# Balanced branches on TensorE, one scatter for four experts' third places, a tenth chunk buffer and another order at the end

## The chip, the cores and the metric

The kernel runs on one core of a Trainium2 chip. The metric is the time of one execution on the device in microseconds; three runs of the kernel before gave 696.25, 698.2 and 699.58 us, median 698.2.

## What is computed

The input is one sequence of 256 tokens with 1024 features, in float32. A first block of two hybrid layers is followed by a second block: a mixer (state-space scan and attention), a layer norm, a mixture of experts and a last layer norm. Only the mixture of experts and the last norm matter here. Each token goes to two of the four experts of one of four groups, 16 experts in all, and an expert is a gated product of 1024 to 512 and back:

```python
def _hier_moe(h, rg_w, rg_b, re_w, re_b, w_gate, w_up, w_down):
    ...
    weights = g_val[:, None] * e_val
    expert_id = g_idx[:, None] * EXPERTS_PER_GROUP + e_idx
    combine = jnp.sum(jax.nn.one_hot(expert_id, N_EXPERTS, dtype=jnp.float32) * weights[..., None], axis=1)
    out = jnp.zeros((bsz * s, d), jnp.float32)
    for e in range(N_EXPERTS):
        act = jax.nn.silu(hf @ w_gate[e]) * (hf @ w_up[e])
        out = out + combine[:, e:e + 1] * (act @ w_down[e]).astype(jnp.float32)
    ...
    # in second_block, behind it:
    h = _layer_norm(DEEPNORM_ALPHA * h + ffn, ln2_g[l], ln2_b[l])
```

## The kernel before, in words

The last third of the program is the expert stage. An expert's tokens are given places: 64 in a first part, 32 in a second, called the third 32 places, and more in a far branch (`further`, L1823) that is entered when any expert has over 96. A one-hot matrix `oh` of a group (128 tokens x 384 places for each half of the sequence: four experts' first 64 places each, then four times 32) is made by `picks` on VectorE. `gather` multiplies the normed tokens, split into two parts, by it and so makes `xg`, the transposed inputs of a group's four experts; `spread` transposes `oh` into `oT` (two ScalarE copies, three blocks: the places of experts 0 and 1, of 2 and 3, and the third 32 of all four), and `scatter` multiplies `oT` by the weighted outputs and adds to the four PSUM banks `acc` of the result. `weights` makes the routing weight of each place by 12 small fp32 products.

Expert e (e = 4q + j, group q, place j in it) goes through these steps. `gate_up` (L1701, called from it) multiplies 32 places by two weight chunks of 2 MB into one PSUM bank, 32 matmuls; a second bank for places 32 to 63 and a third for 64 to 95 are made under `tc.If` on the expert's count (L1726, L1728). `activate` adds the halves, applies Silu and multiplies on ScalarE and VectorE (L1740 to L1744), bank by bank. `turn` (L1762) transposes the result and VectorE copies it to `aT`. `down` multiplies by a third chunk (L1708 for 64 places, L1701 for 32), one expert later: the down of e stands behind the gate_up of e+1. `take` (L1800 to L1803, L1770) copies the result to `y`, and `split_all` (L1810, L1811) weighs it and splits it into two parts for the scatter, for two experts at a time. If the count is over 64 (L1779), `down` first turns the third 32 places in a small transpose, multiplies them, takes, splits and scatters them half by half, and then goes on with the 64 places. From the timeline's rows e4 and e8 have three banks, e0, e2, e6, e10 and e12 two, the others one, and no expert has over 96 places.

The order is written out by hand in `experts`, and each engine runs its instructions in that order. At j = 1 `spread` and the scatter of the group before stand behind gate_up; at j = 2 `weights` of the next group; at j = 3 the scatter of the first pair and `gather_all` for the next group. A `tc.If` without an Else raises on the skipped path the same semaphores that the taken path would have raised, after the engine's own work is done. Weight chunks come over one DMA queue issued by SyncE into a ring of nine buffers (`add_ring`, `load`, `give_back`); a buffer's next load is issued once its last reader is through. At the end stand `further`, the down of e15, the last scatter and the layer norm (L1968 and on).

Of the kernel before, what the change touches and what calls it, by code (L numbers as in the profile page):

```python
# [21 lines left out]
HALF = 512  # L22
# [224 lines left out]
class Net:  # L247
# [1254 lines left out]
    def router(self):  # L1502
# [57 lines left out]
        self.comb = K.tile([P, NT, 16], F32, name="comb")  # L1560

        def weights():
# [7 lines left out]
            by_group(self.comb, ee)  # L1570
        self.pos = K.tile([P, NT, 16], F32, name="pos")
# [22 lines left out]
        nc.scalar.activation(w[:, 0:4:3], w[:, 0:4:3], AF.Exp)  # L1594
        V.tensor_mul(self.pos, ps[:, 0:32].rearrange("p (t e) -> p t e", t=NT), asg)
        self.cnt = K.tile([P, 17], I32, name="cnt")
# [4 lines left out]
        V.tensor_reduce(self.cnt[:, 16:17], self.cnt[:, 0:16], axis=AX, op=OP.max)  # L1601
# [28 lines left out]
    def weights(self, q, oh):  # L1630

        nc, o = self.nc, oh.bitcast(F32)
# [5 lines left out]
        w = self.mw.tile([P, 3, 5], F32, name="wq", bufs=2)  # L1638
        nc.vector.tensor_mul(w[:, :, 0:4], ps[:, 0:12].rearrange("p (c j) -> p c j", c=3), self.c("own", 3, 4))
        nc.vector.tensor_reduce(w[:, :, 4], w[:, :, 0:4], axis=AX, op=OP.add)  # L1640
        return w[:, :, 4]
# [28 lines left out]
    def scatter_all(self, oT, last=False):  # L1670
        for h in range(2):
            self.scatter(oT, [a[:, HALF * h:HALF * h + HALF] for a in self.y], h, last=last)

    def residual(self):
# [17 lines left out]
        self.y2 = [self.mw.tile([P, HALF], F32R if n else F32, name=f"y2{n}") for n in range(3)]  # L1692
        nc.gpsimd.memset(self.y[0], 0.0)

# [15 lines left out]

    def gate_up(self, e):
# [10 lines left out]
        banks = self.gus = [self.gu, self.mbank("s"), self.mbank("s")]  # L1722
        if e + 1 < N_EXP:
            self.count(e + 1)
        self.product32(banks[0], w, KT, x(64 * j))
        with tc.If(self.n[e] > 32):  # L1726
            self.product32(banks[1], w, KT, x(64 * j + 32))
            with tc.If(self.n[e] > 64):  # L1728
                self.product32(banks[2], w, KT, x(256 + 32 * j))
        self.give_back(*rs)  # L1730

    def activate(self, e):
# [13 lines left out]
        with tc.If(self.na[e] > 32):  # L1746
            act(self.gus[1], self.sg[32:64, :], 1)
            with tc.If(self.na[e] > 64):
                act(self.gus[2], self.sg2[0:32, :], 1)

    def count(self, e):
        E = mybir.EngineType
# [273 lines left out]
```

## Time and profile before

| what | value |
|---|---|
| median of three runs | 698.2 us |
| profiled execution | 696.77 us |
| its span in the profile | 695.0 us |
| TensorE busy | 626.3 us, 90% |
| VectorE busy | 451.6 us, 65% |
| ScalarE busy | 306.8 us, 44% |
| mean DMA rate | 236 GB/s |
| mean granted TensorE clock | 0.96 of full speed |

The span begins with the first instruction and ends with the last output's landing; 1.8 us of the execution's time lie around it. All engines run side by side, so a busy share says little by itself. What is to be read is, stage by stage, which engine has no idle time left, and for each of its waits who ended it. The granted clock is that of TensorE's array: at half clock the same matmul row takes nearly twice as long.

### The profile page before, as it was taken

Reading aid. Unit: us, or ns where it says so; the run is one execution under the profiler, and the core shown is the slowest. Engines: PE = TensorE matmul, PEld = TensorE weight load, DVE = VectorE, ACT = ScalarE, POOL = GpSimd, SP = SyncE. Lnnn points to the kernel's source line nnn. Section 1 sums busy time; section 2 is a strip of 40 time slices with the busy share of each in tenths; the row PEclk is TensorE's granted clock in tenths of the full one; section 3 lists DMA queues with packets and bytes.
Section 4 is the critical chain, followed back from the end, with each engine's and each line's share of the span. In section 5 each row is a group of like instructions: output and inputs, shape, how many; then the busy total and the mean of one; then the engine's idle time right before and its main releaser. Section 6 shows DMA issues by size and latency. Waiting matters only on the chain. (4 is left out here: it accounts for less than half of the span.)

```text
span 695.0 us, 11796 instructions
## 1 busy us (share of the span) xinstructions
PE 626.3 (90%) x4466; PEld 443.4 (64%) x4466; DVE 451.6 (65%) x1064; ACT 306.8 (44%) x601; POOL 6.3 (1%) x28
## 2 busy tenths in 40 slices
PE   7999999899899999999999989878979897999762
PEld 4799878688897887898888866523533442363211
DVE  5898767777986777796859877634334433443426
ACT  6764554567545645534646424323332332233321
POOL 1000000000000000000000000000000000000001
PEclk9999999999999999999989998989998998899986
DMA  8956223234452033663305169799999999799821
GB/s 318 426 182 241 112 104 122 92 126 177 165 220 103 5 122 122 273 256 123 123 27 198 56 241 387 282 379 430 421 413 379 371 421 426 280 428 413 333 66 60
DMA packets 15920, 163.68 MB, mean 236 GB/s; under 512 B 1888, under 2 KB 2144, under 8 KB 6624
## 3 DMA queue, kind: packets, MB, share of 16 engines
q1 hardware_dynamic: 15552, 161.84, 58.4%
q8 instruction: 48, 0.79, 0.4%
q10 hardware_dynamic: 288, 0.79, 0.3%
q14 instruction: 32, 0.26, 0.1%
HBM read 161.57 MB, written 1.05 MB: 234 GB/s over the span
## 5 line engine op out<-in xcount | busy, mean ns | idle before, releaser
L318 ACT ACTIVATE whi<-wchunk 128x1024 fp32r<-128x1024 f32 (+2 forms) x103 | 107.4, 1043 | 94.6 <-PE pj L420 49.5
L319 DVE TENSOR_TENSOR wlo<-wchunk,whi 128x1024 fp32r<-128x1024 f32 (+2 forms) x103 | 123.0, 1197 | 18.8 <-ACT whi L318 18.5
L419 PE MATMUL pj<-xh,whi 128*128 128x256 f32 (+1 forms) x440 | 126.8, 289 | 0.0
L420 PE MATMUL pj<-xl,whi 128*128 128x256 f32 (+1 forms) x440 | 126.3, 287 | 0.0
L421 PE MATMUL pj<-xh,wlo 128*128 128x256 f32 (+1 forms) x440 | 125.2, 285 | 0.0
L419 PEld LDWEIGHTS pj<-xh,whi 128*128 128x128 f32 (+1 forms) x440 | 82.5, 188 | 3.2 <-issue 2.2
L420 PEld LDWEIGHTS pj<-xl,whi 128*128 128x128 f32 (+1 forms) x440 | 82.7, 188 | 2.9 <-issue 1.9
L421 PEld LDWEIGHTS pj<-xh,wlo 128*128 128x128 f32 (+1 forms) x440 | 82.7, 188 | 1.8 <-issue 1.6
L1701 PE MATMUL gu<-wchunk,xg 128*32 128x512 f32 x512 | 60.1, 611 | 0.8 <-issue 0.5
L1741 DVE TENSOR_TENSOR tg<-tg,gu 64x256 f32<-64x256 f32 x32 | 13.2, 412 | 46.5 <-ACT tg L1740 46.4
L420 PE MATMUL pj<-wlo,xh 128*128 128x512 f32 (+2 forms) x112 | 40.3, 360 | 1.6 <-DVE wlo L319 1.6
L419 PE MATMUL pj<-whi,mh 128*128 128x512 f32 x96 | 38.5, 404 | 2.6 <-ACT mh L510 2.1
L420 PE MATMUL pj<-wlo,mh 128*128 128x512 f32 x96 | 38.1, 398 | 2.5 <-DVE wlo L319 2.5
L419 PE MATMUL pj<-whi,xh 128*128 128x512 f32 (+2 forms) x112 | 39.1, 355 | 1.1 <-ACT whi L318 1.1
L421 PE MATMUL pj<-whi,xl 128*128 128x512 f32 (+2 forms) x112 | 39.9, 356 | 0.0
L421 PE MATMUL pj<-whi,ml 128*128 128x512 f32 x96 | 37.5, 400 | 0.0
L1701 PEld LDWEIGHTS gu<-wchunk,xg 128*32 128x32 f32 x512 | 15.6, 112 | 32.9 <-issue 32.0
L1667 PE MATMUL acc<-y,oT 128*128 128x512 f32 (+1 forms) x80 | 26.9, 470 | 9.1 <-ACT y L1810 7.7
L1740 ACT ACTIVATE tg<-gu 64x256 f32<-64x256 f32 x32 | 12.1, 379 | 52.1 <-PE gu L1701 31.6
L553 ACT ACTIVATE prob<-bank,smst 128x128 f32<-128x128 f32 (+1 forms) x64 | 26.1, 419 | 18.4 <-DVE smst L551 18.4
L1708 PE MATMUL dn<-wchunk,aT 128*64 128x512 f32 x112 | 28.9, 663 | 4.8 <-PEq L1779 2.8
L1701 PE MATMUL mbs<-wchunk,xg 128*32 128x512 f32 x288 | 32.2, 592 | 0.0
(404 smaller groups left out, 1045.1 us busy)
## 6 DMA issues: line engine op xcount, KB each, us to landing
wchunk<-wstream SPq DMA_DIRECT2D x67, 2048.0 KB, 11.2
wchunk<-wstream SPq DMA_DIRECT2D x12, 512.0 KB, 14.2
wchunk<-wstream SPq DMA_DIRECT2D x2, 1536.0 KB, 9.8
wchunk<-wstream SPq DMA_DIRECT2D x2, 1024.0 KB, 8.4
wchunk<-wstream SPq DMA_DIRECT2D x4, 436.0 KB, 5.6
wchunk<-wstream SPq DMA_DIRECT2D x1, 1744.0 KB, 6.6
wchunk<-xt SPq DMA_DIRECT2D x4, 256.0 KB, 5.3
X<-x SPq DMA_DIRECT2D x4, 256.0 KB, 5.8
```

Of the source, the lines that this page charges most:

```text
L318: nc.scalar.activation(hi, w, AF.Copy)
L319: nc.vector.tensor_sub(lo, w, hi.bitcast(F32))
L419: mm(out, ah, bh, start=start, stop=False)
L420: mm(out, ah, bl, start=False, stop=False)
L421: mm(out, al, bh, start=False, stop=stop)
L553: nc.scalar.activation(p[:, e, j, :N], S[e][:, j, :], AF.Exp, bias=nm[:, e, j:j + 1], accum_out=sm[:, e, j:j + 1])
L1667: self.nc.tensor.matmul(self.acc[t][h], oT[r, t * P:(t + 1) * P], y[1 + i], start=False, stop=last and i == 1, **at)
L1701: self.nc.tensor.matmul(out[r:r + 32, :], lhs(k), w(k)[:, HALF * i:HALF * i + HALF], start=(k < 2), stop=(k >= n - 2), tile_position=(0, r))
L1708: self.nc.tensor.matmul(out[64 * i:64 * i + 64, :], lhs(k), w(k)[:, HALF * i:HALF * i + HALF], start=(k == 0), stop=(k == n - 1), tile_pos ...
L1740: nc.scalar.activation(tg[0:64, 0, s], b[64:128, s], AF.Copy)
L1741: V.tensor_add(tg[0:64, 0, s], tg[0:64, 0, s], b[0:64, s])
```

## The change

- On TensorE every `If` in `gate_up`, `down` and the new `third` gets an Else. It holds one-column products of zeros with the same weight buffers (`none`), so that both paths raise equal signals. Counts are loaded for TensorE apart from ScalarE and VectorE, which no longer take part in TensorE's branches.
- `turn` transposes 96 rows at once instead of 64, and ScalarE makes the copy `aT`, in two buffers.
- The third 32 places: `third` multiplies them behind the turn of the next expert, `take_third` puts them into their rows of `y2` (one tile for a group), and at j = 1 of the next group `split_third` and one scatter treat all four experts' thirds, if any expert of the group has over 64. For TensorE, an Else with four small products stands in for the scatter. Those of e14 and e15 and of the last group go to `further`, which is now entered over 64 in the last group or over 96 anywhere.
- `spread` moves from j = 1 to behind the first activation for e0, and to j = 2, behind gate_up, in later groups. The second scatter of a group stays at j = 1. `take(e - 1)` stands behind `turn(e)`; the chunk is given back behind the third; the scatter of the first pair stands behind the turn.
- `weights` is done for each group at the end of `gather_all`, with a split pair `comb2` in fp32r. `picks` moves to j = 2. The Silu table is loaded in the router.
- Three buffers are added to the ring instead of two: ten in all.
- At the end: the clears of WARM[3] go to `dn`, straight behind the gate_up of e15; `further` stands behind the down and the take of e15; the take splits each half when it has it; the statistics run by halves.

```diff
@@ router
+        nc.scalar.activation(mv[:, 0, 6:7], mv[:, 0, 0:1], AF.Silu)
...
+        V.tensor_reduce(self.cnt[:, 17:21], self.cnt[:, 0:16].rearrange("p (q j) -> p q j", q=4), axis=AX, op=OP.max)
+        V.scalar_tensor_tensor(self.cnt[:, 16:17], self.cnt[:, 16:17], -32.0, self.cnt[:, 20:21], op0=OP.add, op1=OP.max)
@@ weights
-                nc.tensor.matmul(ps[:, 4 * c:4 * c + 4], o[:, t, P * c:P * c + P], self.comb[:, t, 4 * q:4 * q + 4],
+                nc.tensor.matmul(ps[:, 8 * c:8 * c + 8], oh[:, t, P * c:P * c + P], self.comb2[:, t, q],
@@ gate_up
+    def none(self, b, w):
+        self.nc.tensor.matmul(b[:, 0:1], self.zero, w.bitcast(BF16)[:, 1:2], start=True, stop=True)
...
-        with tc.If(self.n[e] > 32):
+        with tc.If(self.n[e] > 32) as more:
             self.product32(banks[1], w, KT, x(64 * j + 32))
-            with tc.If(self.n[e] > 64):
+            with tc.If(self.n[e] > 64) as much:
                 self.product32(banks[2], w, KT, x(256 + 32 * j))
+            with much.Else():
+                none(2)
+        with more.Else():
+            none(1)
+            none(2)
@@ turn
-        aT = self.mw.tile([P, 4, 64], F32, name="aT")
-        nc.vector.tensor_copy(aT.rearrange("p a n -> p (a n)"), ps[:, 0:256])
+        aT = self.mw.tile([P, 4, n], F32, name="aT", bufs=2)
+        nc.scalar.activation(aT.rearrange("p a n -> p (a n)"), ps[:, 0:4 * n], AF.Copy)
@@ third, take_third, split_third
+        b = self.mbank("s")
+        with self.tc.If(self.n[e] > 64) as more:
+            self.product32(b, lambda k: wd[:, k, :], 4, lambda k: aT[:, k, 64:96])
+        with more.Else():
+            self.none(b, wd[:, 0, 0:1])
...
+        with self.tc.If(n > 64):
+            self.nc.scalar.activation(self.t3, b[64:128, :], AF.Copy)
+            for h in range(2):
+                self.add32(b, h, self.y2[32 * j:32 * j + 32, HALF * h:HALF * h + HALF])
...
+        for h in range(2):
+            self.split_rows([self.y2] + y, slice(0, P), slice(HALF * h, HALF * h + HALF), self.wq[q][:, 2:3])
@@ experts, for each e
-            if j == 1:
-                if q:
-                    self.scatter_all(oT[:, 1, :])
+            if j == 1 and q:
+                self.scatter_all(oT[:, 1, :])
+            if j == 2 and q:
                 oT = self.spread(self.oh)
...
             self.activate(e)
+            if e == 0:
+                oT = self.spread(self.oh)
+            if last:
+                for _ in range(WARM[3]):
+                    self.clear(self.dn)
+            a0, aT = aT, self.turn(e)
             if e and not last:
                 self.take(e - 1)
+                b = self.third(e - 1, a0, wd(w))
+                self.give_back(r)
+                self.take_third(e - 1, b, self.na[e - 1])
+            if j == 1 and q:
+                with self.tc.If(naq > 64):
+                    self.split_third(q - 1, self.y[1:])
+                with self.tc.If(nq > 64) as much:
+                    self.scatter_all(oT[:, 2, :])
+                with much.Else():
...
-        self.further()
         w, r = self.load()
...
-        self.down(N_EXP - 1, aT, wd(w), oT)
-        self.take(N_EXP - 1)
-        self.split_all(slice(64, P), self.wq[NQ - 1][:, 1:2])
+        self.down(N_EXP - 1, aT, wd(w))
+        self.take(N_EXP - 1, True)
+        self.further(free, left, oT)
         self.scatter_all(oT[:, 1, :], last=True)
@@ moe
-            self.add_ring(2)
+            self.add_ring(3)
```

Three places in the engines' order show it. The first is TensorE behind the gate/up products of e1 (`mbs` is a bank, `dn` the down bank; the chunks are `wchunk`; in the kernel after, the products of L1701 and L1708 stand at L1714 and L1721, the turn of L1762 at L1789). Before, to the start of the down of e0:

```order
L1701 MATMUL mbs<-wchunk_4569,xg 32x512 x8
L1728 UNCONDITIONAL_BRANCH
L1728 UNCONDITIONAL_BRANCH [waits PE_49]
L1726 UNCONDITIONAL_BRANCH [waits PE_49]
L1626 MATMUL dn<-cstm,oh 128x128 x4
L1626 MATMUL dn<-cstm,oh 128x128 [waits Activation_49]
L1626 MATMUL dn<-cstm,oh 128x128
L1778 COMPARE_AND_BRANCH
L1779 COMPARE_AND_BRANCH
L1781 MATMUL dn<-cstm,sg_4848 128x32 [waits DVE_49,Activation_49]
L1781 MATMUL dn<-cstm,sg_4848 128x32 x3
```

After, at the same place:

```order
L1714 MATMUL mbs<-wchunk_4569,xg 32x512 x8
L1749 UNCONDITIONAL_BRANCH
L1726 LDWEIGHTS zero [waits PE_49]
L1726 MATMUL mbs<-wchunk_4525,zero 128x1 [waits Activation_49]
L1726 LDWEIGHTS zero
L1726 MATMUL mbs<-wchunk_4569,zero 128x1
L1749 UNCONDITIONAL_BRANCH
L1726 LDWEIGHTS zero
L1726 MATMUL mbs<-wchunk_4569,zero 128x1 [waits PE_49]
L1726 LDWEIGHTS zero [waits PE_49]
L1726 MATMUL mbs<-wchunk_4525,zero 128x1 [waits Activation_49]
```

The jumps that wait for TensorE's own semaphore (PE_49) are gone, small products of `zero` stand in the skipped paths, and the six transposes of `spread` (`dn` from `oh`) stand no longer there.

The second is TensorE at the down of e4, in e5. Before, from the product of the third 32 places to the 64:

```order
L1701 MATMUL dn<-wchunk_5352,aT_5878 32x512 [waits DMAHW2_49,DVE_49]
L1701 MATMUL dn<-wchunk_5352,aT_5878 32x512 x7
L1667 MATMUL acc_4835<-y_4923,oT 128x512 [waits Activation_49]
L1667 MATMUL acc_4835<-y_4924,oT 128x512 [waits DVE_49]
L1667 MATMUL acc_4837<-y_4923,oT 128x512
L1667 MATMUL acc_4837<-y_4924,oT 128x512
L1667 MATMUL acc_4836<-y_4923,oT 128x512 [waits Activation_49]
L1667 MATMUL acc_4836<-y_4924,oT 128x512 [waits DVE_49]
L1667 MATMUL acc_4838<-y_4923,oT 128x512
L1667 MATMUL acc_4838<-y_4924,oT 128x512
L1779 UNCONDITIONAL_BRANCH
L1779 UNCONDITIONAL_BRANCH [waits PE_49]
```

After, from the turn of e5 on, with the down of e4 just ahead of it:

```order
L1789 MATMUL mbs<-cstm,sg 128x96 [waits DVE_49,PE_49,Activation_49]
L1789 MATMUL mbs<-cstm,sg 128x96 x3
L1828 COMPARE_AND_BRANCH
L1714 MATMUL mbs<-wchunk_5299,aT 32x512 [waits PE_49,Activation_49]
L1714 MATMUL mbs<-wchunk_5299,aT 32x512 x7
L1828 UNCONDITIONAL_BRANCH
L1726 LDWEIGHTS zero [waits PE_49]
L1726 MATMUL mbs<-wchunk_5299,zero 128x1 [waits Activation_49]
L1828 UNCONDITIONAL_BRANCH
L1814 UNCONDITIONAL_BRANCH
L1836 UNCONDITIONAL_BRANCH
L1998 UNCONDITIONAL_BRANCH
```

The third's product now stands behind the turn of e5, outside the down, and the scatter has become one under a branch of its own (the next rows, L2000).

The third is ScalarE at e6, from the end of e5's branches to the activation of e6. Before:

```order
L1779 UNCONDITIONAL_BRANCH [waits Activation_49]
L1778 UNCONDITIONAL_BRANCH
L1778 UNCONDITIONAL_BRANCH [waits Activation_49]
L1740 ACTIVATE tg<-gu 64x256 [waits DVE_49,PE_49,Activation_49]
L1740 ACTIVATE tg<-gu 64x256 [waits DVE_49]
L1743 ACTIVATE tg<-tg 32x256
L1743 ACTIVATE tg<-tg 32x256 [waits DVE_49]
L1746 COMPARE_AND_BRANCH
L1740 ACTIVATE tg<-mbs 64x512 [waits DVE_49,PE_49,Activation_49]
```

After:

```order
L1782 TENSOR_LOAD cnt
L1782 ISA x2
L1747 UNCONDITIONAL_BRANCH
L1637 ACTIVATE oT<-dn 128x512 [waits DVE_49,PE_49]
L1637 ACTIVATE oT<-dn 128x256 [waits PE_49]
L1766 ACTIVATE tg<-gu 64x256 [waits Activation_49]
L1766 ACTIVATE tg<-gu 64x256 [waits DVE_49]
L1769 ACTIVATE tg<-tg 32x256
L1769 ACTIVATE tg<-tg 32x256 [waits DVE_49]
L1772 COMPARE_AND_BRANCH
L1766 ACTIVATE tg<-mbs 64x512 [waits DVE_49,Activation_49]
```

The two copies of `spread` now stand ahead of the activation (`tg` from `gu`), and ScalarE no longer goes through the branches of `down` there.

## Rows read from the trace of the kernel before

**Rows 1.** Windows; columns: five engines busy, clock granted, DMA share, GB/s:

```profile
440.00:460.00 20.00, 14.21 (x112) 5.42 (x112) 9.06 (x16) 3.98 (x7) 0.95 (x1) 0.83 0.93 383
...
520.00:540.00 20.00, 16.86 (x92) 5.60 (x92) 8.42 (x18) 5.70 (x13) 0.00 (x0) 0.83 0.87 356
...
580.00:600.00 20.00, 16.18 (x74) 5.45 (x78) 6.52 (x14) 4.49 (x9) 0.00 (x0) 0.74 0.86 355
...
660.00:680.00 20.00, 11.82 (x67) 3.83 (x67) 6.58 (x12) 5.30 (x10) 0.00 (x0) 0.83 0.17 57
680.00:695.00 15.00, 3.48 (x8) 2.12 (x7) 9.90 (x19) 0.25 (x1) 2.34 (x12) 0.63 0.19 70
```

**Rows 2.** SyncE's queue: longest wait, and the chunk loads issued:

```profile
SPq L292 <- PE dn L1708: 55.1, 6, 19.7
L292 SPq DMA_DIRECT2D wchunk<-wstream x47: 327/328/1039, 437.0 to 648.3; - x47
```

**Rows 3.** Timeline of TensorE, e0 to e2: start us, us, work [idle before it]:

```profile
441.62 3.64 PE L1701 MATMUL gu<-wchunk,xg 128*32 128x512 f32 x32 [0.27 <-DVE wq L1639]
...
454.05 0.66 PE L1762 MATMUL mbs<-cstm,sg 64*128 64x64 f32 x4 [5.36 <-DVEq L1748]
454.88 5.48 PE L1701 MATMUL gu<-wchunk,xg 128*32 128x512 f32 x32 [0.17 <-issue]
460.55 0.63 PE L1626 MATMUL dn<-cstm,oh 128*128 128x128 f32 x4 [0.19 <-PEq L1726]
...
462.82 3.65 PE L1708 MATMUL dn<-wchunk,aT 128*64 128x512 f32 x16 [0.52 <-ACTq L1779]
...
466.79 3.64 PE L1701 MATMUL gu<-wchunk,xg 128*32 128x512 f32 x32
470.25 3.62 PE L1701 MATMUL mbs<-wchunk,xg 128*32 128x512 f32 x32
```

**Rows 4.** The same timeline, behind skipped banks of e2, e3 and e5:

```profile
474.89 1.93 PE L1701 MATMUL dn<-wchunk,aT 128*32 128x512 f32 x16 [1.03 <-ACT tg L1740]
...
484.18 3.65 PE L1708 MATMUL dn<-wchunk,aT 128*64 128x512 f32 x16 [1.97 <-PEq L1779]
...
512.41 2.10 PE L1667 MATMUL acc<-y,oT 128*128 128x512 f32 x8 [0.18 <-PEq L1726]
```

**Rows 5.** The same timeline, e4's third inside its down:

```profile
508.59 3.64 PE L1701 MATMUL gu<-wchunk,xg 128*32 128x512 f32 x32
...
516.55 0.43 PE L1781 MATMUL dn<-cstm,sg 32*128 32x32 f32 x4 [0.47 <-ACT oT L1627]
...
526.24 5.66 PE L1708 MATMUL dn<-wchunk,aT 128*64 128x512 f32 x16
...
532.22 3.64 PE L1701 MATMUL gu<-wchunk,xg 128*32 128x512 f32 x32
```

**Rows 6.** Timelines of TensorE and VectorE, the tail:

```profile
661.97 3.64 PE L1701 MATMUL gu<-wchunk,xg 128*32 128x512 f32 x32
...
672.89 1.01 PE L599 MATMUL dn<-zero 128*128 128x512 bf16 x2 [3.02 <-PEq L1823]
673.84 3.52 PE L1701 MATMUL dn<-wchunk,aT 128*32 128x512 f32 x16
...
682.95 1.89 DVE L1968 BATCH_NORM_STATS2 bst<-acc 128x6 f32<-128x512 f32 x3 [1.01 <-PE acc L1667]
```

**Rows 7.** Groups from 440 us: work, count, busy us, mean ns, idle:

```profile
L1811 DVE SCALAR_TENSOR_TENSOR y<-y,wq,y 128x512 fp32r<-128x512 f32 x14 | 9.9, 747 | 0.1
...
L1636 PE MATMUL mbs<-comb,oh 128*128 128x4 f32 x48 | 6.0, 254 | 0.1
...
L1740 ACT ACTIVATE tg<-mbs 64x512 f32<-64x512 f32 x9 | 5.3, 593 | 11.3 <-PE mbs L1701 5.5 <-PEq L1728 5.2 <-DVE sg L1744 0.7
...
L1627 ACT ACTIVATE oT<-dn 128x512 fp32r<-128x512 f32 x4 | 2.4, 597 | 19.4 <-PE dn L1626 19.4
...
L1743 ACT ACT_TABLE_LOAD x1 | 1.3, 1283 | 0.0
```

More of the change, by code (lines that the diff above doesn't have):

```diff
@@ L1668, in scatter, with scatter_all @@
                                       stop=last and i == 1, **at)
-    def scatter_all(self, oT, last=False):
+    def scatter_all(self, oT, last=False, y=None):
         for h in range(2):
-            self.scatter(oT, [a[:, HALF * h:HALF * h + HALF] for a in self.y], h, last=last)
+            self.scatter(oT, [a[:, HALF * h:HALF * h + HALF] for a in y or self.y], h, last=last)
     def residual(self):
@@ L1691, in residual @@
         self.t3 = self.tg[64:128, 0, :]
-        self.y2 = [self.mw.tile([P, HALF], F32R if n else F32, name=f"y2{n}") for n in range(3)]
+        self.y2 = self.mw.tile([P, D], F32, name="y2")
         nc.gpsimd.memset(self.y[0], 0.0)
+        nc.gpsimd.memset(self.y2, 0.0)
     def product32(self, out, w, n, lhs):
@@ L1722, in gate_up, with none @@
         banks = self.gus = [self.gu, self.mbank("s"), self.mbank("s")]
+        def none(i):
+            for a in ws[2 - i:]:
+                self.none(banks[i], a[:, 0, 0:1])
         if e + 1 < N_EXP:
@@ L1875, in places @@
         V.tensor_copy(aT, b.rearrange("p (i s) -> p i s", i=4))
-        y = self.y2
+        y = [None] + [self.y3[:, HALF * i:HALF * i + HALF] for i in range(2)]
         for h in range(2):
@@ L1902, in gather_all @@
                 self.gather(self.oh, S["xg"], k)
-                if k == KT - 1 and not self.wq:
-                    self.wq[0] = self.weights(0, self.oh)
+                if k == KT - 1:
+                    self.wq[len(self.wq)] = self.weights(len(self.wq), self.oh)
         gather_all()
@@ L1927, in experts @@
                 w, r = self.load()
-                self.down(e - 1, aT, wd(w), oT)
-                self.give_back(r)
+                self.down(e - 1, aT, wd(w))
             self.activate(e)
+            if e == 0:
+                oT = self.spread(self.oh)
+            if last:
+                self.tc.mark_branch_hint_location("further", "LikelyTaken")
+                for _ in range(WARM[3]):
+                    self.clear(self.dn)
+            a0, aT = aT, self.turn(e)
             if e and not last:
                 self.take(e - 1)
-            if j == 1 and more:
-                self.oh = self.picks(q + 1)
-            if j == 3 and more:
-                self.scatter_all(oT[:, 0, :])
-            if j == 2 and more:
-                self.wq[q + 1] = self.weights(q + 1, self.oh)
-            if last:
-                self.tc.mark_branch_hint_location("further", "LikelyTaken")
-                self.warm(WARM[3])
-            aT = self.turn(e)
+                b = self.third(e - 1, a0, wd(w))
[7 more added lines that the diff above has]
+                with much.Else():
+                    for h in range(2):
+                        for y in self.y[1:]:
+                            self.nc.tensor.matmul(self.acc[1][h][:, 0:1], self.zero,
+                                                  y.bitcast(BF16)[:, h * D + 1:h * D + 2], start=False, stop=False)
             if j == 2:
+                if more:
+                    self.oh = self.picks(q + 1)
                 self.split_all(slice(0, P), self.wq[q][:, 0:1])
@@ L1965, in last_norm @@
         mv = m.tile([P, NT, 8], F32, name="mv2")
-        for t in range(NT):
-            for h in range(2):
+        for h in range(2):
+            for t in range(NT):
                 V.bn_stats(st[:, t, h, :], self.acc[t][h])
```

98 lines of the change are left out of this document (59 added, 39 removed).

## Prediction

> **What bounds the kernel now.** I read the windows first: which engine fills its time, and where [rows 1]. From 440 us on, in the expert stage, TensorE is busy 12 to 17 of the 20 us of these windows (up to 19 in those not shown), VectorE and ScalarE under 10. The DMA share of 0.86 to 0.93 looks like a bound too, so the next look is at who waits for whom on the queue that loads: SyncE waits for buffers that TensorE has not yet given back, 55.1 us for one line alone [rows 2]. Loads run ahead and are held up by TensorE, not the other way. So the time of the stage is TensorE's program order, and TensorE's rows with the idle time in brackets are to be added up. Everything ahead of 430 us is the same in both kernels but for a table load. After the last BatchNorm statistics come 10.2 us that the change leaves alone.
>
> Call "step of e" the time from the start of expert e's gate/up products to that of e+1. At full clock a bank (32 rows in TensorE) takes 3.45 us (the bank of 466.79 is followed by the next at 470.25; the row's 3.64 overlaps it), a 64-row down 3.6, a 32-row down 1.9, one scatter of 128 places 2.1 [rows 3 to 5].
>
> **Part 1: equal signals by Else.** Before, a skipped bank or third ends in a jump that waits for TensorE's own earlier work; behind it stand gaps of 0.17 to 1.97 us. Three of them stand in [rows 4]; from 458 to 654 us there are fourteen such rows, 10.2 us in all. ScalarE's activation of second banks also waited 5.2 us for such jumps (PEq L1728 in [rows 7]). In the order of after the waiting jumps are gone and a dummy of one column stands in each Else. But TensorE then arrives sooner at the turn (the transposes of the activated rows), which needs ScalarE and VectorE: four operations of 0.59 (ScalarE [rows 7]), 0.68, 0.63 and 0.68, so 2.6 us for a second bank, against 1.9 of down in between: 0.8 is left as waiting at an expert with a 32-row down ahead. Where the down has 64 rows some 0.4 stays.
>
> **Part 2: the routing weights** are now made in fp32r at the end of every gather: 12 small products of 1.5 us [rows 7] leave the steps of e2, e6, e10 (and the start), and 6 cheaper ones go into e3, e7, e11. No row has an fp32r product of that size: bounds 0 and 1.5 (no cheaper than now); I take half, for half the count, 0.7.
> So e2: 1.03 (gap) + 1.43 - 0.8 = 1.6 gained; e3: 1.97 - 0.4 - 0.7 = 0.9; e12: 0.6; e7 and e11 lose 0.2 each; the stage starts 1.0 earlier. Together **+3.7**.
>
> **Part 3: e0 and e1.** The step of e0 is 13.26, with 5.36 of waiting for the activation [rows 3]. The table load of 1.28 in it [rows 7] goes to the router, where ScalarE idles; with the shorter branch end I count 1.7. The permutation's transposes (spread, 460.55 to 462.82, 2.3 with its waits) move from e1 into e0's wait. And e1's product takes 5.48 instead of 3.64, since the granted clock fell behind the long wait [rows 3] (0.83 for 440 to 460 in [rows 1]). e1: 11.91 to 7.7, 4.2 gained. Together **+5.9**.
>
> **Part 4: the third 32 places** of e4 and e8. Before, one runs inside the down of e4: from 516.55 to 526.24, 9.7 us of small products and waits, and the 64-row down behind it takes 5.66 at half clock instead of 3.65 [rows 5]. The step of e5 is 23.6 (508.59 to 532.22), that of e9 24.9. After: 3.45 + 2.05 + 0.4 (scatter and its wait) + 3.57 + 0.5 + 1.86 (third) and 2.3 of waiting, because the dummies of the skipped scatter need VectorE to have taken the third (0.59 + 2 x 0.68 and the latencies): 14.5. In e9 the scatter is taken: 2.05 more, and a wait of 3.3 for the split (VectorE 0.75 for each half [rows 7], ScalarE about the same ahead of it): 17.45. Gains 9.1 and 7.5. e4 and e8 themselves lose 1.1 each: turn now holds 96 rows and waits for the third bank's activation. e13 pays for the scatter of e8's group: 2.05 + 3.3, less the 2.2 of spread that leaves it: -3.6. Together **+10.8**.
>
> **Part 5: spread at j = 2**, behind gate/up of e6, e10, e14. Its two ScalarE copies, 0.60 and 0.38 [rows 7], stand ahead of the activation there, so the activation of two banks starts when they are done, and TensorE waits some 3.5 at the turn. e6: 11.7 - 1.4 - 0.9 + 2.05 + 3.5 = 15.0, so -3.3; e10 -3.2; e14 -2.1 (it skips the second bank, but the copy of the turned rows stands late on ScalarE). Together **-8.6**. This part is bounded by 0 (if ScalarE and VectorE catch up during the down) and -11 (three times 3.6).
>
> **Part 6: the tail.** The jump over the far code cost 3.02 ahead of e15's down [rows 6], and the step before it, the clears and the turn, waited for the activation. After, the jump stands behind the take, and the clears fill that wait: gate/up to down takes 7.4 instead of 11.9. From the down on it gets longer: the halves are taken and split in turn (+1.4), and VectorE has its own jump ahead of the statistics; its price isn't in a row of this stretch, so I take TensorE's 3.02, between 0 (hidden behind the last scatter) and 4.7. Against that stands 2.9 for the half clock (3.52 [rows 6] against 1.93 [rows 4] for the down, so 1.6, and 1.3 for the last scatter behind it), counted as returned here. Together **+3.0**.
>
> **The tenth buffer**: 0. One more buffer only lets loads run further ahead, and they are held by TensorE [rows 2]: 0 on both sides while that holds; rival (d) has the case in which it doesn't. The added sums over the counts on VectorE lie beside the gather.
>
> **The sum** at full clock: 3.7 + 5.9 + 10.8 - 8.6 + 3.0 = 14.8 us.
>
> **The clock** comes off this. The granted clock has two levels here; in the stage it fell to half behind e0's wait, in both thirds and in the tail (0.83, 0.83, 0.74, 0.83, 0.63 [rows 1]), always behind a wait or a run of small products between waits. Behind the wait of 1.97 in [rows 4] the down ran at full rate (3.65). I counted its returns above (some 10 us). But after has its own sparse stretches: e0 (3 us of waiting), e5, e9 and e13 (2.3 to 3.3, behind small products), e6 and e10 (3.5), the tail. One fall costs 1.84 under a gate/up product [rows 3], 2.0 under a 64-row down [rows 5], 1.7 in the tail. Bounds: none, and all seven, 13 us. I take four: 3 x 1.84 + 1.7 = 7.2. [...]
>
> So the profiled run goes from 696.8 (span 695.0 and 1.8 around it) to 696.8 - 14.8 + 7.2 = 689.2. The median of the three runs stands 1.4 above the profiled run; I carry that over: **690.6 us**.
>
> **Rivals.**
> (a) *The jumps themselves are the cost, not the waiting in them: slower.* Place: TensorE's branches in gate/up, down and the new third. If code behind a skipped block comes late whatever stands there, the fourteen gaps (10.2) stay, and twelve skipped thirds add one each at their mean of 0.73, 8.8. It decides from about half that price on. For it: 3.02 for the far jump in a row. Against it: a gate/up skip shows only 0.18 when a scatter follows [rows 4], and the 1.97 gap ends with a drain that the order names. Time: 690.6 + 10.2 - 4 (the waits at the turn that these gaps would cover) + 8.8 = 705.6; at half that price 698.1. [...]
> (b) *The clock stays up and VectorE's jump is hidden.* No fall in the stage and 3 less in the tail: 690.6 - 7.2 - 3.0 = 680.4. For it: the two longest waits are gone. Against: e6 and e10 get new ones.
> (c) *Moves cancel: no change.* Spread and split waits at their upper bounds and all seven falls: 698.2 - 14.8 + 13 + 2.4 = 698.8. For it: the serial chains through ScalarE and VectorE are longer than any cover in [rows 5].
> (d) *The loads bind: no other sign.* If the last chunk could not come sooner than now (issued at 648.3 [rows 2], 14.1 us to land by the median of that line, so 662.4), e15's down could not start before that; the sum has it at 657.6 without falls and at 663 with three of them ahead. So it takes up to 5 us of (b) and nothing of the forecast.
>
> **How the numbers follow.** Forecast (two to six falls, 684 to 695) 0.55; (b) 0.15; (c) 0.17; (a) 0.13. The range leaves out the deeper end of (b) and the upper half of (a): 680 to 700. About 0.5%, 3.5 us, is what a measurement of this kernel can tell from no change. Faster: the forecast and (b), and a little of (c): 0.72. Same: most of (c): 0.15. Slower: (a) and the rest: 0.13.
>
> **What would show it.** In the profile after: no row "PEq" of over 0.5 ahead of a down in e2, e3, e7, e11 (Part 1); step of e5 near 14.5 and of e9 near 17.5 (Part 4); in e6 and e10 a wait of about 3.5 at the turn, ended by VectorE (Part 5); down of e15 straight behind the clears, with a VectorE gap ahead of the statistics (Part 6); falls of the granted clock in four of 20 us windows. I'm wrong on the whole if gaps stand ahead of dummies (a), or if the clock column is below 0.85 in more than five windows of the stage (c).

## The result, and the profile after

| | before | after |
|---|---|---|
| median of the runs | 698.04 us (4 runs) | 709.26 us (4 runs, 708.88 to 710.42) |
| profiled execution, span | 696.77, 695.0 us | 709.35, 707.6 us |
| ratio of the times | | 1.0165, interval 1.0137 to 1.0192 |

The kernel became 1.6% slower, where 690.6 us, 1.1% faster, had been forecast, with a range of 680 to 700. Up to the first gate/up product nothing moved: it starts at 441.62 before and 441.64 after. From there to the end of the last statistics (684.84 before, 697.39 after) the stage takes 12.5 us more, and behind it nothing changed. So the whole difference lies where the prediction summed it, and its steps can be checked one by one. A step of e is again the time from the start of one expert's gate/up products to the next's.

The windows of after, to be read against [rows 1]: five engines' busy us, the granted clock, the DMA share and the rate.

```profile
500.00:520.00 20.00, 15.38 (x103) 5.40 (x93) 7.84 (x13) 7.46 (x14) 0.00 (x0) 0.91 1.01 426
520.00:540.00 20.00, 12.68 (x97) 4.14 (x96) 4.37 (x8) 4.39 (x9) 0.00 (x0) 0.91 1.01 427
...
560.00:580.00 20.00, 15.71 (x128) 5.33 (x121) 7.14 (x12) 6.50 (x12) 0.00 (x0) 0.86 0.72 293
...
600.00:620.00 20.00, 14.88 (x102) 4.73 (x96) 8.51 (x18) 7.84 (x16) 0.00 (x0) 0.83 0.83 335
...
640.00:660.00 20.00, 16.63 (x89) 7.25 (x92) 6.53 (x11) 6.36 (x12) 0.00 (x0) 0.83 0.71 282
```

TensorE is busy 12.7 to 16.6 us of these 20, and the clock column is below 1 in each; from 500 to 620 all six windows stand at 0.83 to 0.97. Of the ten windows of 20 us from 460 to 660, seven are below 1 here; before, two were [rows 1]. Two things went wrong, then: TensorE waits more, and it runs slower behind the waits. The timeline of TensorE shows both (start us, duration us, work, and in brackets the idle time before it and what ended it). First e3, where the forecast came true, then e4 and the first product of e5:

```profile
476.91 3.65 PE L1721 MATMUL dn<-wchunk,aT 128*64 128x512 f32 x16
...
492.94 7.08 PE L1714 MATMUL mbs<-wchunk,xg 128*32 128x512 f32 x64
499.81 1.93 PE L1714 MATMUL dn<-wchunk,aT 128*32 128x512 f32 x16
505.72 0.52 PE L1789 MATMUL mbs<-cstm,sg 96*128 96x96 f32 x4 [3.98 <-DVE sg L1770]
...
506.91 4.98 PE L1714 MATMUL gu<-wchunk,xg 128*32 128x512 f32 x32 [0.57 <-issue]
```

The down at 476.91 follows the gate/up product at once; its counterpart in [rows 4] waited 1.97. But at 505.72 the turn of e4 waits 3.98 for VectorE, where 0.8 was forecast, and the gate/up product behind it takes 4.98 instead of 3.64. ScalarE shows where the 3.98 comes from:

```profile
494.53 0.87 ACT L1769 ACTIVATE tg<-tg 32x256 f32<-32x256 f32 x2
500.09 0.59 ACT L1766 ACTIVATE tg<-mbs 64x512 f32<-64x512 f32 x1 [4.69 <-PE mbs L1714]
...
502.89 0.59 ACT L1766 ACTIVATE tg<-mbs 64x512 f32<-64x512 f32 x1 [0.83 <-DVE sg L1770]
```

The second bank's product begins at 492.94 and the third's follows in the same row, so that by 3.45 a bank the second is ready at 496.4. ScalarE touches it only at 500.09, when the third is ready too. Both banks' chains then stand one behind the other after the last product. In e8 it is the same (569.11).

Then e6 and e7, e8's end and e9, and e14:

```profile
533.91 1.92 PE L1714 MATMUL dn<-wchunk,aT 128*32 128x512 f32 x16 [0.47 <-ACT oT L1637]
539.45 0.52 PE L1789 MATMUL mbs<-cstm,sg 96*128 96x96 f32 x4 [3.61 <-DVEq L1774]
...
540.56 5.22 PE L1714 MATMUL gu<-wchunk,xg 128*32 128x512 f32 x32 [0.57 <-issue]
...
574.73 0.87 PE L1789 MATMUL mbs<-cstm,sg 96*128 96x96 f32 x4 [3.99 <-DVE sg L1770]
...
575.91 6.32 PE L1714 MATMUL gu<-wchunk,xg 128*32 128x512 f32 x32 [0.30 <-issue]
...
653.72 4.14 PE L1679 MATMUL acc<-y,oT 128*128 128x512 f32 x8 [2.73 <-ACT y L1849]
...
670.64 3.32 PE L1714 MATMUL dn<-wchunk,aT 128*32 128x512 f32 x16 [2.67 <-ACT y L1849]
```

The turn of e6 waits 3.61 (3.5 forecast). Behind nearly every such wait a product runs slow: 5.22 at 540.56, where 0.50 of the clock is granted from 541 to 543, and 6.32 at 575.91. And the tail, on TensorE and VectorE:

```profile
682.43 0.52 PE L1789 MATMUL mbs<-cstm,sg 96*128 96x96 f32 x4 [1.81 <-DVEq L1772]
...
683.53 3.48 PE L1714 MATMUL dn<-wchunk,aT 128*32 128x512 f32 x16
```

```profile
694.90 2.49 DVE L2037 BATCH_NORM_STATS2 bst<-acc 128x6 f32<-128x512 f32 x4 [2.75 <-DVEq L1862]
```

The down of e15 now follows without a code jump (3.02 in [rows 6]), and VectorE waits 2.75 ahead of the statistics for its own (3.02 assumed); the down still runs at half clock, 3.48 instead of 1.92 (0.50 granted from 684 to 687).

### The profile page after: what moved, and what is told of

Its sections match the earlier page's. It is cut to its first block, busy times and chain, and to the rows that moved or that the text cites. A ratio compares the mean times of both kernels' runs of the same rounds, so it can differ in the third digit from the quotient of the medians.

```text
span 707.6 us, 11743 instructions
## 1 busy us (share of the span) xinstructions
PE 630.5 (89%) x4487; PEld 445.7 (63%) x4487; DVE 445.2 (63%) x1050; ACT 314.5 (44%) x618; POOL 7.2 (1%) x29
## 5 line engine op out<-in xcount | busy, mean ns | idle before, releaser
L1714 PE MATMUL gu<-wchunk,xg 128*32 128x512 f32 x512 | 69.6, 692 | 4.5 <-issue 3.5
L1714 PEld LDWEIGHTS gu<-wchunk,xg 128*32 128x32 f32 x512 | 17.8, 125 | 44.7 <-issue 43.5
L1679 PE MATMUL acc<-y,oT 128*128 128x512 f32 x80 | 25.0, 454 | 8.5 <-ACT y L1849 7.3
L1714 PE MATMUL mbs<-wchunk,xg 128*32 128x512 f32 x288 | 32.3, 592 | 0.0
L1789 PE MATMUL mbs<-cstm,sg 96*128 96x96 f32 x64 | 9.6, 278 | 20.0 <-DVEq L1774 9.4
## 6 DMA issues: line engine op xcount, KB each, us to landing
wchunk<-wstream SPq DMA_DIRECT2D x67, 2048.0 KB, 11.3
```

Of the source, the lines that this page charges most:

```text
L1679: self.nc.tensor.matmul(self.acc[t][h], oT[r, t * P:(t + 1) * P], y[1 + i], start=False, stop=last and i == 1, **at)
L1714: self.nc.tensor.matmul(out[r:r + 32, :], lhs(k), w(k)[:, HALF * i:HALF * i + HALF], start=(k < 2), stop=(k >= n - 2), tile_position=(0, r))
L1789: nc.tensor.transpose(ps[:, n * i:n * i + n], self.sg[p, P * i:P * i + P], self.ident[p, p])
```

## The experiments

All but two of the kernels are edits of the changed kernel; the medians stand beside 709.3 for it and 698 for the kernel before. Some profiles enter the stage 1.5 us later than others, so steps are compared within the stage.

### Which count ScalarE waits for

The first theory was that ScalarE's wait for the second bank comes from the counts being loaded for TensorE alone.

```diff
-        self.n[e] = self.nc.values_load(c, engines=(E.PE,), min_val=0, max_val=T)
+        self.n[e] = self.nc.values_load(c, engines=(E.PE, E.Activation, E.DVE), min_val=0, max_val=T)
```

> The changed kernel, with the counts loaded for TensorE, ScalarE and VectorE together again (as before), so that ScalarE and VectorE follow TensorE's branches. Theory J (with counts for TensorE alone, ScalarE's second bank must wait for the end of TensorE's whole branch, and so for the third bank's product): in e4 and e8 the second bank's activation starts 3.4 us earlier, the wait ahead of the turn falls from 3.98 to under 1.2, and e4 and e8 give back 3 each; with the half-clock products behind them (1.3 and 2.7 in e5 and e9) up to 10: 698 to 704 us against 709.3. Rival (something else holds that activation, or the added branches on ScalarE and VectorE cost as much): 708 to 711.

Measured: 712.0 us (2 runs), and the turn of e4 waits 3.99. The theory fell: who follows the branch doesn't matter for this wait. The next try was the Else of gate_up by itself, in the kernel before:

```diff
-        with tc.If(self.n[e] > 32):
+        with tc.If(self.n[e] > 32) as more:
             self.product32(banks[1], w, KT, x(64 * j + 32))
-            with tc.If(self.n[e] > 64):
+            with tc.If(self.n[e] > 64) as much:
                 self.product32(banks[2], w, KT, x(256 + 32 * j))
+            with much.Else():
+                none(2)
+        with more.Else():
+            none(1)
+            none(2)
```

> The kernel before with the Else of gate_up alone (counts for all three engines as before, nothing else of the change). Prediction's Part 1: the gaps behind skipped banks (0.17 to 1.03, some 6 us without those of the down's branch) go and half of it comes back as waiting for the activation at the turn: 694 to 696 us against 698.0. Rival (a) (the jumps cost, not the drain): 698 to 701.

Measured: 717.4 us (2 runs), 19 over the kernel before and far beyond either expectation. ScalarE's row for the second bank of e4, whose product starts at 498.90 and so ends at 502.4, and TensorE's row at the down in e11:

```profile
506.03 0.59 ACT L1752 ACTIVATE tg<-mbs 64x512 f32<-64x512 f32 x1 [4.69 <-PE mbs L1701]
```

```profile
626.22 6.61 PE L1708 MATMUL dn<-wchunk,aT 128*64 128x512 f32 x16 [4.03 <-PEq L1791]
```

The late activation is there too, with counts for all three engines: it belongs to the nested Else. How the built program counts tells why. (These numbers are read from the semaphore instructions of the built program, not from a trace.) Both paths of the branch raise TensorE's semaphore by the same sum, 32. On the taken path the second bank's last product adds 16, the third bank's products 14, 1 and 1. In the Else of the outer branch the one dummy of the second bank adds 30, the two of the third 1 each. A reader of the second bank must wait for a count that holds on either path, and 30 is reached on the taken path only in the last matmuls of the third bank (16 and 14). ScalarE's instruction does wait for the count behind the first bank plus 30. The second row shows another loss, of which more below: a wait of 4.03 for TensorE's own sequencer at the skipped third.

If that is it, the cure is to put the branches one behind the other, so that each path of the first adds 16:

```diff
         with tc.If(self.n[e] > 32) as more:
             self.product32(banks[1], w, KT, x(64 * j + 32))
-            with tc.If(self.n[e] > 64) as much:
-                ...
-        with more.Else():
-            none(1)
-            none(2)
+        with more.Else():
+            none(1)
+        with tc.If(self.n[e] > 64) as much:
+            self.product32(banks[2], w, KT, x(256 + 32 * j))
+        with much.Else():
+            none(2)
```

> The changed kernel, with the two branches of gate_up one behind the other instead of one inside the other, each with its own Else. Theory N (in the nested form the dummy of the second bank adds 30 to TensorE's count, which the taken path reaches only in the third bank's product, so ScalarE waits for the third bank before it touches the second): now both paths of the first branch add 16, the second bank's activation in e4 and e8 starts 3.4 earlier, the turn's wait of 3.98 falls to under 1.2, and with the half-clock products behind it (1.3 and 2.7) 8 to 10 us come back: 699 to 702 us against 709.3. Rival (one more branch at every expert with a single bank costs a code fetch each): 704 to 712.

Measured: 703.2 us (2 runs), 6.1 less. ScalarE's second bank and TensorE's turn in e4, and the product behind it:

```profile
498.23 0.59 ACT L1765 ACTIVATE tg<-mbs 64x512 f32<-64x512 f32 x1 [1.29 <-PE mbs L1714]
```

```profile
504.53 0.52 PE L1788 MATMUL mbs<-cstm,sg 96*128 96x96 f32 x4 [1.25 <-DVE sg L1769]
...
505.72 3.64 PE L1714 MATMUL gu<-wchunk,xg 128*32 128x512 f32 x32 [0.66 <-issue]
```

The product of that bank starts at 494.48 and ends at 497.9, and ScalarE takes it at once. The turn waits 1.25 instead of 3.98, and the next product runs at full clock, 3.64 instead of 4.98. The steps: e4 17.40 to 14.67, e8 17.39 to 14.70, e5 16.00 to 14.66. In the built program ScalarE now waits for the first bank's count plus 16. That settles the theory. The 703.2 lies just above the expected 699 to 702, because e9 gave nothing back (19.32 and 19.30). Its product takes 3.64 instead of 6.32, but TensorE then waits between the dummies of the two branches, and the scatter at the end of e9 runs slow (2.4 for its two rows in the changed kernel):

```profile
576.18 0.21 PE L1726 MATMUL mbs<-wchunk,zero 128*128 128x1 bf16 x2 [1.33 <-ACT tg L1765]
...
586.64 3.83 PE L1679 MATMUL acc<-y,oT 128*128 128x512 f32 x8 [2.38 <-ACT y L1848]
```

A wait between the two dummies is what the rival of this run had named, the price of one more branch. In this trace it stands at one of the nine experts with a single bank, not at each.

### What the Else is worth

With the same kernel, but no Else in gate_up and the waiting jumps in their place:

```diff
-        with tc.If(self.n[e] > 32) as more:
+        with tc.If(self.n[e] > 32):
             self.product32(banks[1], w, KT, x(64 * j + 32))
-            with tc.If(self.n[e] > 64) as much:
+            with tc.If(self.n[e] > 64):
                 self.product32(banks[2], w, KT, x(256 + 32 * j))
-            with much.Else():
-            ...
```

> The changed kernel, with gate_up's branches as before the change (no Else, waiting jumps on the skipped paths; all other branches keep theirs). Theory N: e4 and e8 give the same 8 to 10 us back as with the branches one behind the other; the waiting jumps return at nine single-bank and five two-bank experts, where TensorE's next code waits 0.2 to 2.5 us: 700 to 706 us. Prediction's Part 1 (the Else is worth 4 to 6 us by itself): 712 to 716.

Measured: 708.3 us (2 runs), a bit above the range of theory N. Against 703.2 with the branches in a row, the Else in its good form is worth 5.1 us, within the 4 to 6 that this expectation took from Part 1. In its nested form it gains nothing: 709.3 against 708.3, a difference too small to count.

In the kernel before, the Else in its good form (the diff as above, for before):

> The kernel before with gate_up's two branches one behind the other, each with its Else, and nothing else of the change. Theory N: against the nested Else in the same kernel (717.4) the second bank of e4 and e8 is read 3.4 us sooner, 3 to 6 us of it reach the end; what stays above the kernel before's 698 is the waiting jump at down's skipped third, which TensorE now meets with an empty queue (4.0, 2.6 and 2.5 us in e11, e7 and e3 with the nested Else, 0.95, 0.87 and 1.97 before): 706 to 713 us. Prediction's Part 1 taken alone: 692 to 696.

Measured: 707.7 us (2 runs), in the range of theory N and 10 above the kernel before. The down's product in e3 and e7, where the third is skipped by the old waiting jump:

```profile
486.67 5.35 PE L1708 MATMUL dn<-wchunk,aT 128*64 128x512 f32 x16 [3.77 <-PEq L1790]
...
556.25 5.33 PE L1708 MATMUL dn<-wchunk,aT 128*64 128x512 f32 x16 [3.74 <-PEq L1790]
```

TensorE's sequencer keeps it waiting 3.77 and 3.74, where [rows 4] has 1.97 for e3 and the kernel before has 0.87 for e7, and the down behind runs at 5.35 instead of 3.65:

```profile
548.43 3.65 PE L1708 MATMUL dn<-wchunk,aT 128*64 128x512 f32 x16 [0.87 <-PEq L1779]
```

The two-bank steps e2, e6 and e10 became 0.8 to 1.0 shorter, as Part 1 says; e3, e7 and e11 became 3.6, 4.7 and 3.9 longer. In e11 it isn't the jump. The down begins after 0.37 and stops behind three of its sixteen products, for nothing that the profile names:

```profile
620.88 1.04 PE L1708 MATMUL dn<-wchunk,aT 128*64 128x512 f32 x3 [0.37 <-ACT tg L1751]
623.95 4.92 PE L1708 MATMUL dn<-wchunk,aT 128*64 128x512 f32 x13 [2.03 <-issue]
```

So here the Else alone didn't pay; in the changed kernel, which also took the old jump out of down, it did. What TensorE waits for there is not settled by an experiment. The DMA view of 483.5 to 485.0, inside the wait of e3, has one packet on a queue that brings instructions (16 KB each: in the kernel before, 48 of them move 0.79 MB in the span), in a stretch where the chunk loads fill the DMA engines (queue, packets, MB, share of the engines):

```profile
q1 hardware_dynamic: 49, 0.66, 104.5%
q8 instruction: 1, 0.02, 4.1%
```

In the kernel before the whole stage from 440 to 640 has 18; none lies inside the 1.97 of e3 (482.2 to 484.2), the last one just ahead of it (481 to 482.2). That fits rival (a), code that isn't there yet, without showing it: the view doesn't tell which engine a packet is for.

### Where the spread stands

```diff
-            if j == 2 and q:
+            if q and j == (2 if q == NQ - 1 else 3):
                 oT = self.spread(self.oh)
```

with the next group's `picks` moved to the same expert, since it overwrites the matrix that spread reads.

> The changed kernel, with the spread of groups 1 and 2 moved one expert on, behind the gate/up of e7 and e11, where one bank is activated and a 64-row down of 3.6 us follows (the one-hot matrix for the next group is then made there too). Theory S (the two copies ahead of a two-bank activation make the wait of 3.6 at the turn of e6 and e10): those waits fall to about 1, steps of e6 and e10 shorten by 2 + 2.6 each, e7 and e11 grow by 2, and their half-clock products (1.6 and 2.1) come back: 699 to 704 us. Rival (the chain on ScalarE only moves along to e7 and e11): 707 to 711.

Measured: 703.1 us (8 runs, 699.6 to 707.3), 6.1 less. The turn of e6 and the product of e7, then the down of e6 and the turn of e7:

```profile
534.94 0.52 PE L1789 MATMUL mbs<-cstm,sg 96*128 96x96 f32 x4 [1.09 <-DVEq L1774]
...
536.15 3.64 PE L1714 MATMUL gu<-wchunk,xg 128*32 128x512 f32 x32 [0.68 <-issue]
...
542.04 3.65 PE L1721 MATMUL dn<-wchunk,aT 128*64 128x512 f32 x16 [0.47 <-ACT oT L1637]
545.63 0.55 PE L1789 MATMUL mbs<-cstm,sg 96*128 96x96 f32 x4
```

The wait at the turn falls from 3.61 to 1.09 and the product of e7 runs at full clock, 3.64 instead of 5.22. In e7 the spread hides the activation: its turn doesn't wait at all. Steps: e6 17.65 to 13.06, e10 16.05 to 11.81, e7 17.96 to 18.52, e11 18.40 to 19.00. The profile is that of the fastest of the eight runs, so its steps give back more than the median does.

### What the clock costs

```diff
+    def busy(self, n):
+        b = self.acc[0][0].rearrange("p (a n) -> p a n", a=4)
+        for _ in range(n):
+            self.nc.tensor.matmul(b, self.zero, self.zero[:, None, :].to_broadcast([P, 4, P]), start=False, stop=False)
...
+            if j in (0, 2) and q and not last:
+                self.busy(12)
             a0, aT = aT, self.turn(e)
...
+                self.busy(6)
                 with self.tc.If(nq > 64) as much:
```

> The changed kernel, with 12 products of zeros (2.6 us) added to the result ahead of the turn of e4, e6, e8, e10, e12 and e14, and 6 ahead of the third scatter in e5, e9, e13: they add nothing to the result and lie in waits of 2.3 to 4.0 us. Theory C (the waits cost twice, since the granted clock falls behind them): the gate/up products of e5, e6, e7, e9 and e11 take 3.64 again instead of 5.0 to 6.3, 7 to 9 us together, less up to 3 where the zeros are longer than the wait (e12, e14): 701 to 705 us. Rival (the clock follows something else than TensorE's waits): products as slow as now, 709 to 713.

Measured: 700.0 us (8 runs), 9.3 less and 1 under the expected range, though nothing but work was added. TensorE at the end of e8 and in e9, to be read against 574.73 and 575.91 of after:

```profile
569.47 2.76 PE L1859 MATMUL acc<-zero 128*128 128x512 bf16 x12
573.52 0.52 PE L1789 MATMUL mbs<-cstm,sg 96*128 96x96 f32 x4 [1.29 <-DVE sg L1770]
...
574.62 3.64 PE L1714 MATMUL gu<-wchunk,xg 128*32 128x512 f32 x32 [0.56 <-issue]
```

The turn comes no sooner after the down (it still ends a wait for VectorE), but the gate/up product takes 3.64 instead of 6.32. The products of e6, e7, e9, e11 and e14 all take 3.64 again; only e1 (5.25) and e5 (5.34) don't. e12 and e14 lose 0.5 and 0.9, where the zeros are longer than the wait.

### The far branch

```diff
         left.append((e, aT, wd(w)))
+        self.further(free, left, oT)
...
         self.take(N_EXP - 1, True)
-        self.further(free, left, oT)
```

> The changed kernel, with the far branch back ahead of the down of e15. Prediction's Part 6 has the far jump at 3.0 on TensorE ahead of the down, and at 3.0 on VectorE ahead of the statistics in its new place (2.75 read since): the move is worth nothing, 708 to 711 us. Rival (in its new place it is hidden for TensorE and only half exposed for VectorE): 711 to 713.

Measured: 711.2 us (2 runs), at the lower end of the rival's range and just above the other. TensorE at the clears ahead of the down, and VectorE's statistics:

```profile
687.12 1.01 PE L599 MATMUL dn<-zero 128*128 128x512 bf16 x2 [4.86 <-PEq L1862]
```

```profile
696.10 2.58 DVE L2037 BATCH_NORM_STATS2 bst<-acc 128x6 f32<-128x512 f32 x4
```

In the old place the jump costs TensorE 4.86 in this kernel, and VectorE's 2.75 is gone. The step from e15's gate/up to the end of the statistics is 23.43 against 21.46, so the new place is the better one, by 2.0 (1.9 in the medians).

### Repairs together

Branches in a row and the spread at e7 and e11, without zeros:

> The changed kernel with two of the three repairs, the branches one behind the other and the spread of groups 1 and 2 at e7 and e11, without the zeros. If the two add up (6.1 each against 709.3): 697 us, about the kernel before's 698, so that the zeros are what makes the repaired kernel (684.8) faster than before, by 12. If most of the half-clock time goes with the waits themselves (the repaired places were those where the clock fell): 688 to 693.

Measured: 694.8 us (10 runs, 692.8 to 699.5), ratio 0.9972 to the kernel before, interval 0.9947 to 0.9998. That is 14.5 under the changed kernel, 2 more than the two alone add up to, and between the two expectations. Then with zeros in what is left of the waits (`busy` as above; the numbers are those of its products, 8 being ahead of e14's down):

```diff
+                self.busy(8)
...
+            if j in (0, 2) and q and not last:
+                self.busy(4)
...
+                self.busy(6)
```

> The changed kernel with three repairs together: gate_up's branches one behind the other, spread of groups 1 and 2 at e7 and e11, and products of zeros in the waits that are left (4 ahead of the turns of e4, e6, e8, e10, e12 and e14, 6 ahead of the third scatter, 8 ahead of the down of e14). Spread gave 6.1 by itself and the zeros 9.3; the branches should give 8; up to 8 of this is the same half-clock time counted twice or thrice: 691 to 696 us, under the kernel before's 698. If the losses lie elsewhere: 698 to 702.

Measured: 684.8 us (4 runs, 684.1 to 685.6), ratio 0.9814, interval 0.9791 to 0.9837, 6 under the expected range. This version beats both kernels, by 13.3 and 24.5 us. Its windows:

```profile
500.00:520.00 20.00, 17.70 (x129) 6.65 (x125) 7.83 (x13) 6.83 (x13) 0.00 (x0) 1.00 1.00 423
520.00:540.00 20.00, 18.21 (x147) 5.94 (x140) 8.56 (x18) 7.84 (x16) 0.00 (x0) 1.00 1.00 424
...
560.00:580.00 20.00, 17.90 (x114) 7.07 (x106) 9.28 (x15) 7.67 (x15) 0.00 (x0) 1.00 1.00 425
...
600.00:620.00 20.00, 19.93 (x143) 11.60 (x140) 7.94 (x17) 6.46 (x12) 0.00 (x0) 1.00 1.01 427
```

The clock is full in each of the ten windows from 460 to 660, and TensorE is busy 17.7 to 19.9 of 20 us in these four; without the zeros three of the ten were below 1 (0.92, 0.99 and 0.76). The zeros are worth 10.0 in the medians and 7.4 in the profiled spans (691.0 to 683.6). Of the 9.1 by which the steps up to e15 get shorter, some 6 are clock. e6 falls from 12.99 to 11.19, since its own product goes from 5.34 to 3.64. e14 falls from 18.53 to 15.75: its down starts no sooner behind the turn (3.19 in both), but takes 1.92 instead of 3.64. In e13, 16.49 to 15.17, the scatter at its end is faster. But e7 and e9, 1.5 and 1.9 shorter, gain by something else. Without the zeros TensorE waits there between the dummies of gate_up's two branches, as in e9 of the run with the branches in a row:

```profile
536.81 0.21 PE L1726 MATMUL mbs<-wchunk,zero 128*128 128x1 bf16 x2 [1.32 <-issue]
...
571.92 0.21 PE L1726 MATMUL mbs<-wchunk,zero 128*128 128x1 bf16 x2 [1.75 <-DVE tg L1766]
```

The repaired kernel has no such wait. Why is open: the zeros stand behind those dummies, and they also move the code. So the run with zeros in the changed kernel, where no such waits stood, is the cleaner measure of the clock. e15's end stays slow: 3.24 for its down and 3.18 for the last seven products of the scatter, which take 1.92 and 1.90 at full clock, with 0.75 granted from 660 to 674. Last, the same with nine buffers:

```diff
-            self.add_ring(3)
+            self.add_ring(2)
```

> The repaired kernel (684.8) with nine chunk buffers instead of ten. Prediction: the tenth buffer is worth 0 while TensorE holds the buffers: 684 to 686 us. Rival (the loads bind now that TensorE's waits are gone; the DMA share is at 1.0 from 460 to 620): 688 to 693.

Measured: 685.5 us (4 runs, 684.1 to 687.0). The tenth buffer is worth nothing that can be measured, even with a DMA share of 1.00 to 1.01 from 460 to 620 in the repaired kernel.

## Why the prediction was wrong, by its steps

The sum had 14.8 us gained at full clock and 7.2 given back to the clock; 12.5 were lost in the stage. By part, forecast at full clock and measured with all that happened:

| part | forecast | measured |
|---|---|---|
| 1 and 2: e2, e3, e7, e11, e12 and the start | +3.7 | -2.7 |
| 3: e0 and e1 | +5.9 | +5.0 |
| 4: e4, e5, e8, e9 and e13 | +10.8 | -1.2 |
| 5: e6, e10 and e14 | -8.6 | -15.1 |
| 6: from e15's gate/up | +3.0 | +1.4 |

**The failed step is in Part 1**, that an Else costs a dummy of one column and changes nothing else. It changed the count by which the second bank is read, and so put the chain of e4's and e8's second bank behind the third's product. The wait at their turn was 0.8 in the sum and 3.98 in the trace, 3.2 each. The order of after, which shows that waiting jumps are gone, doesn't show for which count a reader waits; it would have had to be taken from the numbers of the counts, not from the names. With the branches in a row 6.1 us came back, part of it as clock.

**The second is a mis-sized term: the clock**, taken as 7.2 and the largest single miss. From the rows, gate/up products of e1, e5, e6, e7, e9, e11 and e14 take 4.60 to 6.32 instead of 3.64, together 11.3; the scatter ahead of e14 (4.14 against 2.09), the downs of e14 and e15 (3.32 and 3.48 against 1.92) and the last scatter add some 6.5: 17.8, ten more than taken. I had counted four falls because the 1.97 of [rows 4] did no harm; the products behind 3.98 (e4) and 3.61 (e6) did run slow. With zeros the time falls by 9.3 in the changed kernel, clock by the products' rows, and by 10.0 in the repaired one, some two thirds of it clock. In the repaired kernel the clock column is 1.00 in all ten windows with the zeros, products without any use, and 0.92, 0.99 and 0.76 in three of them without. How long a wait the clock survives is not shown.

**The third is a wait that was not in the sum**: "issue" ahead of a gate/up product, 0.30 to 0.67 in rows like 506.91, at e3, e5, e6, e7, e9, e11 and e13, 3.5 us in all (0.5 before). By the program's order TensorE's sequencer still has a branch and the load of the next count ahead of it there; that they are the cause is not shown, as no experiment took them out. The three make 6.4, 10.6 and 3.5, together 20.5; forecast and measured stage lie 20.1 apart (7.6 gained, 12.5 lost), so that the smaller misses cancel.

**Sums.** Part 4's terms as printed add up to 14.1 for e5 and 17.2 for e9, where 14.5 and 17.45 are taken, and to 3.15 for e13, where 3.6 is; the start's 1.0 is 0.8 by its own terms (1.5 less 0.7). Put right, the forecast would gain 0.9 us more, which matters little beside the miss.

**Right were** the gaps of Part 1 where nothing else hit (e3 gains 1.15 for 0.9; the down at 476.91 without a gap); Part 3 (the product of e1 at 4.60 for 3.64 is the difference); the structure of Part 4 (e5 16.00 for 14.5 and e9 19.32 for 17.45, both over by the slow product; 14.67 and 16.66 in the repaired kernel); the wait of Part 5 (3.61 for 3.5 at e6 and e10; e14 lost 4.8 for 2.1, of which 2.4 is the slow product, 4.63, and the slow down, 3.32); Part 6 in the price of VectorE's jump (2.75 for 3.02), though the half clock that it counted as returned stayed; and the tenth buffer at 0. The start gained nothing: the weights take 0.83 (0.7 taken) instead of 1.5, but the first product then waits 0.98 for VectorE to read them.

Of the signs, those of Parts 1, 5 and 6 came true. The sign for the clock did not work: falls were to be seen in four windows and are in seven of the ten from 460 to 660, but a column below 0.85 in more than five windows, which was to betray (c), never came, since falls of a few us leave a window of 20 at 0.83 to 0.97.

**The rivals.** Slower it became, but not by (a): the jumps of the changed kernel are mostly hidden, as 476.91 shows. Where a price like that of (a) shows is the kernel before with the Else alone (3.77 at the down in e3), though its cause is not shown. (c) had the right things, the serial chains and all the falls, and reached 698.8; with 3.2 twice for the nested count and 3.5 for "issue" it would have reached 708.7. That this meets the measured 709.3 is partly luck, as its 13 for the falls stands against 17.8. The repaired kernel's 684.8 is no proof of (b)'s 680.4 either: it also has the spread in another place, so that e6 and e10 take 11.2 and 11.4 where Part 5 had 15.0 and 14.9.

## What to carry to other kernels

When the paths of a branch are balanced by an Else, look at which count a reader on another engine waits for: here the dummy that carried the sum of the nested branch, 30, had ScalarE begin the second bank at 500.09 instead of 496.4, with the third. Branches in a row, each balanced by itself, kept that wait at the bank's own product (1.29 instead of 4.69); the second branch cost 1.3 to 1.75 us at one or two experts in two of the kernels, and nothing in the others. Where an engine's waits are cut into many short ones, price each with the slow product behind it, and see whether work without use in the wait is cheaper: here 9.3 us for a few lines in the changed kernel.

## What the runs showed of the hardware

Products of zeros, added to a bank whose value they leave as it is, kept the granted clock at 1.00 in all ten windows from 460 to 660 us. With the same order of work and no zeros three of the ten were below 1 (0.92, 0.99 and 0.76), and in the changed kernel seven (0.83 to 0.97). And the same skipped third ahead of the down cost TensorE 1.97 and 0.87 us in e3 and e7 of the kernel before, and 3.77 and 3.74 when only gate_up, the code ahead of it, had changed; a 16 KB packet of instructions lay inside the longer wait of e3. What ends these waits is not shown: no run here moved code alone.
